# Four edits to a two-layer decoder trunk in emulated fp32: transposes issued together, additions by DMA, two more places with seven products, banks of their own for the last tile

## The chip, the cores and the metric

One core of a Trainium2 chip runs the whole kernel. Its engines are TensorE (PE, with a separate row PEld for loading the stationary operand), VectorE (DVE), ScalarE (ACT), GpSimd (POOL) and SyncE (SP); each executes its own instructions strictly in order. POOL and SP do little here beyond issuing DMAs. A tile framework adds semaphore waits where an instruction needs another engine's result or a buffer that is still being read. The metric is the device time in microseconds of one execution.

## What is computed

256 tokens of width 2048 go through two layers, all in float32. Layer 0 mixes by causal pooling, layer 1 by dilated attention; each is followed by a gated FFN with a causal convolution of width 3 over the tokens. After each part comes a layer norm of the residual sum (post-norm).

```python
def conv_ffn(h, w_up, conv_w, conv_b, w_down):
    u = h @ w_up                                   # 2048 -> 2 * 5504
    up = jnp.pad(u, ((0, 0), (CONV_WIDTH - 1, 0), (0, 0)))
    c = conv_b + up[:, 0:S] * conv_w[0]
    for j in range(1, CONV_WIDTH):
        c = c + up[:, j:j + S] * conv_w[j]
    gate, val = jnp.split(c, 2, axis=-1)
    return (jax.nn.silu(gate) * val) @ w_down      # 5504 -> 2048

for i in range(DEPTH):                             # DEPTH = 2
    mix = pool_mixer(h, ...) if i == 0 else dilated_attention(h, k_shared, v_shared, ...)
    h = layer_norm(DEEPNORM_ALPHA * h + mix, ln1_g[i], ln1_b[i])
    ff = conv_ffn(h, ffn_w_up[i], ffn_conv_w[i], ffn_conv_b[i], ffn_w_down[i])
    h = layer_norm(DEEPNORM_ALPHA * h + ff, ln2_g[i], ln2_b[i])
```

## The kernel before

**Arithmetic.** An fp32 product is made of three products of rounded halves: each operand is split into a high part and the rest, and high·high, high·low and low·high are accumulated. Activations are split once per tile; weights are split as they stream in: ACT casts the high part (`wh`, L99), DVE subtracts to get the low part (`wl`, L100).

**Units.** The program is a list of 435 units, mostly one 512 x 512 block of weights (1 MB) each. `run_units` (L141) does for each unit, in this order: loads up to 5 units ahead and splits up to 3 ahead (`ahead`, L126), copies registered for this unit (`before`), the unit's matmuls, then work that was put off to this unit with `later(n, fn)` (n units on), and the unit's own ending. SP issues all weight loads, into 3 buffers; 4 buffers hold split weights. This program order is the order on every engine, so what a post or a late function issues stands in front of later splits on ACT and DVE.

**The start.** `x_quad` (L532) turns one quarter of x (512 channels) from token-major to channel-major by 8 PE transposes in two halves of 4; after each half ACT copies (L547) and DVE subtracts (L548) to split it, and a copy of H is put off to a later unit. The two halves share one tile of two PSUM banks. Quads 1 to 3 are read in the middle of the first units of `add_in(3)`; quad 0 is read before them, its two halves by separate calls.

**Norms.** With the second norm of layer 0, `shift` (L381) computes the mean over channels of the first part of the residual with PE, ACT copies it to SBUF (L385), and `less` (L405) subtracts it from H[1] to H[3] on DVE, one quarter per unit, H[0] in `one`. Then residual sums arrive (L337), statistics S and Q are collected by DVE (L363 to L369), and `chain` (L424) sums both over the partitions by PE at L425 and L426.

**The FFN.** The hidden width is cut in quarters of 512 channels, q = 0 to 10 (the last has 384). For each, a gate and a value group of 4 units go up; `conv` (L607) makes three taps: ACT scales, DVE adds to `c` (L618); then ACT applies Silu one unit later (L640, `three`), and the product with the value is split (`lo_part`, L304). The down projections go in four chunks (quarters 0–2, 3–5, 6–7, 8–10) and four columns c of 512 outputs, token-major, by `group_tm` (L202). A block of it is multiplied either directly (`go_t`: 24 matmuls of 512 columns) or by seven products of half-blocks instead of eight (`mk_seven`: 42 matmuls of 256 columns in two units, "a" and "b"); the table `sevens` says which quarter and column goes which way. For seven products, `split_sums` (L107) has to form sums of weight blocks by DVE (L120 to L124, three more operations) and splits in two pieces (L113, L114), and at the end of such a column `early_post` (L836) combines the sums: by two DMA additions from POOL into `ht` (L286) or, in the last chunk, by five DVE operations. Layer 0 multiplies the last chunk channel-major (`add_last`), so `sevens[9]` matters only in layer 1.

**The end.** In layer 1 the last column, c = 3 of the last chunk, is `apart`: the first 128 tokens are multiplied first and finished (`finish0`), then the other 128 in two halves of 256 columns (`finish1`). Their accumulators are one new bank "t2" and the second bank of the pair "t". PSUM has 4 pairs of banks (`psp`).

**Attention.** `outputs` (L1097) evacuates two heads at once: one ACT copy, one DVE subtraction (L1110).

## Time and profile before

| | us |
|---|---|
| median of 3 runs | 2026.61 (2026.36 to 2027.33) |
| profiled execution | 2028.4 |
| its span, first to last instruction | 2026.6 |
| granted PE clock, mean | 0.998 of full speed |

| engine | idle just before its costliest groups, us | ended by |
|---|---|---|
| DVE, L100 | 174.6 | ACT, L99 |
| ACT, L99 | 169.0 | PE at L180, 74.6 of it |
| ACT, L113 | 194.7 | mostly DVE, L122 |
| POOL, L286 | 1447.0 | mostly DVE, L869 |

In the chain that ended last PE has 97% and DVE 1%. DMA moves 406.72 MB, 201 GB/s on the mean; its slices vary from 166 to 238 GB/s.

How to read the rows that follow. A row of the waits has the engine and what it was about to run, what it waited for, the total in us, the number of waits and the longest one. A row of the timeline has the start and the duration in us, the engine, line, operation, output and inputs with their form, the number of instructions of which the row is made, and in brackets how long the engine was idle before, and for whom. A row of windows has the limits, the length, the busy time of the engine asked for with its number of instructions, the granted clock, the share of the DMA engines and GB/s. A row of groups ends in total busy time, mean ns of one, and idle time before it with the releaser.

### The profile page before, as it was taken

The numbers are of one execution on the slowest core, as the hardware profiler recorded it, in microseconds if no ns is written. First come the engines' busy times: TensorE is split into PE (matmuls) and PEld (weight loads), VectorE is DVE, ScalarE is ACT, GpSimd is POOL, SyncE is SP. The second block draws the span as 40 slices with busy tenths as digits, with TensorE's granted clock in tenths as the row PEclk, the third lists the DMA queues.
The fourth block names the chain that finished last, engine by engine and source line by source line (L and its number), as shares of the span: only waits on it lengthen the run. The fifth ranks groups of instructions, "written<-read, shape, count | busy, mean of one in ns | idle before, by whom it ended". The sixth has DMA issues, their size and how long they took to land.

```text
span 2026.6 us, 31409 instructions
## 1 busy us (share of the span) xinstructions
PE 2010.2 (99%) x12742; PEld 1812.3 (89%) x12742; DVE 1731.8 (85%) x1823; ACT 1268.6 (63%) x1548; POOL 90.4 (4%) x151
## 2 busy tenths in 40 slices
PE   8999999999999999999999999999999999999998
PEld 7898988999899988889898988998899989989987
DVE  5868887999899989879896878787899899989998
ACT  5554686766776686656553444477767677667672
POOL 2000000000000000000000021000000000000000
PEclk9999999999999999999999999999999999999999
DMA  7655567666656758775565666557666756665765
GB/s 232 214 190 199 167 204 208 177 208 222 214 175 220 234 174 238 216 220 170 190 205 167 197 175 207 187 177 218 167 218 202 225 185 220 208 213 183 218 218 166
DMA packets 270241, 406.72 MB, mean 201 GB/s; under 512 B 74398, under 2 KB 84532, under 8 KB 269840
## 3 DMA queue, kind: packets, MB, share of 16 engines
q1 hardware_dynamic: 259488, 388.93, 58.8%
q0 software_dynamic: 10176, 15.13, 5.0%
q8 instruction: 100, 1.64, 0.3%
q10 hardware_dynamic: 432, 0.66, 0.1%
q14 instruction: 45, 0.37, 0.1%
HBM read 380.01 MB, written 2.10 MB: 189 GB/s over the span
## 4 chain that ended last, share of the span: by engine, by line
PE 97%; DVE 1%; issue 0%; DMA 0%; ACT 0%; SPq 0%; DVEq 0%
PE acc L180 43%; PE acc L181 22%; PE s L244 3%; PE s L242 3%; PE s L243 3%; PE acc L184 3%; PE acc L185 3%; PE acc L183 3%; PE t L244 2%; PE t L242 2%; PE t L243 2%; PE t L253 2%; PE t L254 2%; PE t L255 2%; DVE wl L100 0%
## 5 line engine op out<-in xcount | busy, mean ns | idle before, releaser
L180 PE MATMUL acc<-xc,wh 128*128 128x512 f32 x3264 | 1152.1, 396 | 0.0
L181 PE MATMUL acc<-xc,wl 128*128 128x256 f32 x3264 | 916.0, 281 | 0.0
L100 DVE TENSOR_TENSOR wl<-raw,wh 128x2048 fp32r<-128x2048 f32 (+2 forms) x305 | 657.4, 2163 | 174.6 <-ACT wh L99 172.6
L180 PEld LDWEIGHTS acc<-xc,wh 128*128 128x128 f32 x3264 | 616.0, 189 | 143.6 <-issue 0.3
L99 ACT CAST wh<-raw 128x2048 fp32r<-128x2048 f32 (+2 forms) x305 | 548.6, 1805 | 169.0 <-PE acc L180 74.6
L181 PEld LDWEIGHTS acc<-xc,wl 128*128 128x128 f32 x3264 | 615.4, 189 | 0.1
L113 ACT CAST wh<-raw 128x1024 fp32r<-128x1024 f32 x142 | 148.5, 1052 | 194.7 <-DVE raw L122 175.5
L114 DVE TENSOR_TENSOR wl<-raw,wh 128x1024 fp32r<-128x1024 f32 x142 | 169.4, 1222 | 11.2 <-ACT wh L113 11.2
L121 DVE TENSOR_TENSOR wl<-raw,wh 128x1536 fp32r<-128x1536 f32 x71 | 124.5, 1753 | 6.6 <-ACT wh L119 5.6
L119 ACT CAST wh<-raw 128x1536 fp32r<-128x1536 f32 x71 | 104.9, 1477 | 36.8 <-PE acc L180 28.9
L286 POOL DMA_DIRECT2D ht<-w x48 | 41.3, 1014 | 1447.0 <-DVE ht L869 721.9
L244 PE MATMUL t<-wh,g 128*128 128x256 f32 x376 | 105.7, 281 | 0.0
L242 PE MATMUL t<-wh,g 128*128 128x256 f32 x376 | 105.6, 281 | 0.0
L243 PE MATMUL t<-wl,g 128*128 128x256 f32 x376 | 105.4, 280 | 0.0
L612 ACT ACTIVATE c<-u,cv 128x256 f32<-128x256 f32 x172 | 89.5, 592 | 23.0 <-DVE f L674 16.4
L244 PE MATMUL s<-wh,xs 128*128 128x256 f32 x344 | 96.2, 280 | 0.0
L242 PE MATMUL s<-wh,xs 128*128 128x256 f32 x344 | 96.1, 279 | 0.0
L243 PE MATMUL s<-wl,xs 128*128 128x256 f32 x344 | 96.0, 279 | 0.0
L124 DVE TENSOR_TENSOR raw<-raw 128x1024 f32<-128x1024 f32 x71 | 87.0, 1225 | 2.4
L617 ACT ACTIVATE a<-u,cv 128x256 f32<-128x256 f32 x172 | 73.5, 499 | 11.9 <-DVE g L684 11.9
L603 ACT COPY u<-acc 128x512 f32<-128x512 f32 x84 | 46.8, 572 | 47.1 <-PE acc L181 46.8
L617 ACT ACTIVATE u<-u,cv 128x256 f32<-128x256 f32 x172 | 73.4, 499 | 0.0
(328 smaller groups left out, 3440.4 us busy)
## 6 DMA issues: line engine op xcount, KB each, us to landing
raw<-in_ffn_w_up_dram SPq DMA_DIRECT2D x160, 1024.0 KB, 5.2
raw<-in_ffn_w_down_dram SPq DMA_DIRECT2D x80, 1024.0 KB, 5.1
raw<-in_pool_w_out_dram SPq DMA_DIRECT2D x16, 1024.0 KB, 5.0
raw<-in_shared_w_k_dram SPq DMA_DIRECT2D x16, 1024.0 KB, 5.1
raw<-in_attn_w_q_dram SPq DMA_DIRECT2D x16, 1024.0 KB, 5.3
raw<-in_shared_w_v_dram SPq DMA_DIRECT2D x16, 1024.0 KB, 5.2
raw<-in_attn_w_o_dram SPq DMA_DIRECT2D x16, 1024.0 KB, 5.2
ht<-w POOLq DMA_DIRECT2D x50, 256.0 KB, 4.9
```

The lines of the kernel that those rows point to most:

```text
L99: A.copy(wh[i][:, s], r[:, s])
L100: V.tensor_tensor(wl[i][:, s], r[:, s], wh[i][:, s].bitcast(F32), OP.subtract)
L113: A.copy(h[:, :, n], r[:, :, n])
L114: V.tensor_tensor(l[:, :, n], r[:, :, n], h[:, :, n].bitcast(F32), OP.subtract)
L119: A.copy(hs, rs)
L121: V.tensor_tensor(ls, rs, hs.bitcast(F32), OP.subtract)
L180: PE.matmul(ps[m].ap, h[:, k, c], q[:, k, :, :T], start=st, stop=False)
L181: PE.matmul(ps[m][:, :T], l[:, k, c], q[:, k, 0, :T], start=False, stop=sp)
L242: PE.matmul(to, xh, h[:, k, n], start=opens and kk == 0, stop=False)
L243: PE.matmul(to, xh, l[:, k, n], start=False, stop=False)
L244: PE.matmul(to, xl, h[:, k, n], start=False, stop=ends and kk == 1)
L617: A.activation(to[:, m, :], u[:, m, i:i + T], AF.Copy, scale=cv[:, i, j:j + 1])
```

## The change

1. `x_quad` issues all its transposes first and copies the halves afterwards; H is copied by one ACT operation instead of two.
2. `shift` stores the negated mean, in a tile of its own for the norm in question; `less` becomes a DMA issued by POOL that adds the broadcast mean to H[1], H[2] and H[3] in SBUF, straight at `shift`.
3. Layer 0, quarter 7: the line that kept columns 2 and 3 direct is gone, so all four go by seven products.
4. Layer 1, quarter 9: column 1 too goes by seven products (columns 0 to 2; column 3 remains direct).
5. Layer 1, gates of quarters 8 to 10: the third tap is added to `c` by a POOL DMA instead of DVE.
6. The last tile (`apart`): the pair "t" serves the first 128 tokens alone, and each half of the others gets a new bank "th".
7. `outputs`, last group of heads: one copy and one subtraction per head.

```diff
--- before.py
+++ after.py
@@ -207,7 +207,9 @@
 
         def opened():
             t = pair("t")
-            ps.extend([t[:, 0, :], t[:, 1, :]])
+            ps.append(t[:, 0, :])
+            if not apart:
+                ps.append(t[:, 1, :])
             if seven:
                 t = pair("s")
                 ps.extend([t[:, 0, :], t[:, 1, :]])
@@ -258,8 +260,6 @@
             def go(h, l):
                 if j == 0:
                     opened()
-                    if apart:
-                        ps.append(bank("t2"))
                 held.append((h, l, xqs[j]()))
                 if not apart:
                     for t in range(2):
@@ -270,6 +270,7 @@
                     post(0, ps[0])
                     for half in range(2):
                         c = slice(256 * half, 256 * half + 256)
+                        ps.append(bank("th"))
                         for i in range(j + 1):
                             go_t(*held[i], 1, i, ps[1 + half][:, :256], c)
                         post(1, ps[1 + half], half)
@@ -381,13 +382,16 @@
     def shift(s, first, lay, which):
         ps = bank("shift")
         PE.matmul(ps[:, :T], ones4, s, start=True, stop=True)
-        cs = ST["w4"][:, 3:4, :]
-        A.copy(cs[:, 0, :], ps[:, :T])
+        if first:
+            cs = ST["w4"][:, 3:4, :]
+        else:
+            cs = pools["ffn"].tile([P, 2, T], F32, name="cs", tag="xs", bufs=1)[:, 0:1, :]
+        A.activation(cs[:, 0, :], ps[:, :T], AF.Copy, scale=-1.0)
         cb = cs.to_broadcast([P, 4, T])
         ST["S"] = ST["Q"] = None
 
         def one():
-            V.tensor_tensor(H[0], H[0], cb, OP.subtract)
+            V.tensor_tensor(H[0], H[0], cb, OP.add)
             if first:
                 pre(1)
             stats(0)
@@ -399,16 +403,16 @@
                 pre(3)
 
         def pre(q):
-            V.scalar_tensor_tensor(H[q], H[q], ALPHA, cb, op0=OP.mult, op1=OP.subtract)
+            V.scalar_tensor_tensor(H[q], H[q], ALPHA, cb, op0=OP.mult, op1=OP.add)
 
         def less(q):
-            V.tensor_tensor(H[q], H[q], cb, OP.subtract)
+            nc.gpsimd.dma_start(H[q], cb, accum_op=OP.add)
 
         later(1, one)
         later(2, two)
         if not first:
             for q in (1, 2, 3):
-                later(1 + q, lambda q=q: less(q))
+                less(q)
 
     def xp(q, lay, which):
         g0 = 32 * which
@@ -536,17 +540,21 @@
             XC[q] = quad_tile("xc")
         if halves[0] == 0:
             ST["xT"] = pair("xT")
+        both = ST["xT"]
         for half in halves:
-            ps = ST["xT"][:, half, :]
             for kk in range(2):
                 for t in range(2):
                     k = 2 * half + kk
-                    PE.transpose(ps[:, kk * T + t * P:kk * T + t * P + P], xin[q, t][:, k * P:(k + 1) * P], ident)
-            pv2 = ps.rearrange("p (k t) -> p k t", k=2)
+                    PE.transpose(both[:, half, kk * T + t * P:kk * T + t * P + P], xin[q, t][:, k * P:(k + 1) * P],
+                                 ident)
+        for half in halves:
+            pv2 = both[:, half, :].rearrange("p (k t) -> p k t", k=2)
             s = slice(2 * half, 2 * half + 2)
             A.copy(XC[q][:, s, 0, :T], pv2)
             V.tensor_tensor(XC[q][:, s, 1, :T], pv2, XC[q][:, s, 0, :T].bitcast(F32), OP.subtract)
-            before.setdefault(min(q + 1, 3), []).append(lambda s=s, pv2=pv2: A.copy(H[q][:, s, :], pv2))
+        if halves[-1] == 1:
+            before.setdefault(min(q + 1, 3), []).append(
+                lambda: A.copy(H[q], both.rearrange("p b (k t) -> p (b k) t", k=2)))
 
     def add_in(g, mids=()):
         group(pool_w_in[0], rows4, 512 * g, 512, xsrcs, pool_post(g), mode="a" if g == 3 else "ab", mids=mids)
@@ -582,9 +590,7 @@
         sevens = {q: every for q in range(8)}
         sets = {0: "C", 1: "A", 2: "B", 3: "C", 4: "A", 5: "B", 6: "A", 7: "CB"[lay], 9: "A"}
         if lay == 1:
-            sevens[9] = (0, 2)
-        else:
-            sevens[7] = (0, 1)
+            sevens[9] = (0, 1, 2)
         free, done = {}, {}
 
         def pads():
@@ -604,24 +610,27 @@
                 V.tensor_tensor(y, y, p[:, :n, :T], OP.add)
             return u
 
-        def conv(u, blk0, nb, then, quick=False):
+        def conv(u, blk0, nb, then, quick=False, by_dma=False):
             cv = cvec[lay]
             c = pools["ffn"].tile([P, 4, T], F32, name="c", tag="t4")
             for m in range(nb):
                 j = blk0 + m
                 A.activation(c[:, m, :], u[:, m, 2:], AF.Identity, scale=cv[:, 2, j:j + 1], bias=cv[:, 3, j:j + 1])
 
-            def tap(i, to):
+            def tap(i, to, by_dma=False):
                 for m in range(nb):
                     j = blk0 + m
                     A.activation(to[:, m, :], u[:, m, i:i + T], AF.Copy, scale=cv[:, i, j:j + 1])
-                V.tensor_tensor(c[:, :nb], c[:, :nb], to[:, :nb], OP.add)
+                if by_dma:
+                    nc.gpsimd.dma_start(c[:, :nb], to[:, :nb], accum_op=OP.add)
+                else:
+                    V.tensor_tensor(c[:, :nb], c[:, :nb], to[:, :nb], OP.add)
 
             def second():
                 tap(1, pools["ffn"].tile([P, 4, T], F32, name="a", tag="t4"))
 
             def third():
-                tap(0, u[:, :, 0:T])
+                tap(0, u[:, :, 0:T], by_dma)
                 then(c)
 
             for n, fn in ((1, second), (2, third)):
@@ -642,7 +651,7 @@
 
                     later(1, three)
 
-                later(1, lambda: conv(u, 4 * q, nb, gated))
+                later(1, lambda: conv(u, 4 * q, nb, gated, by_dma=lay == 1 and q > 7))
 
 
 
@@ -1106,8 +1115,10 @@
             PE.matmul(ps[:, :T], vt[:, 0, hd], t[:, :T], start=True, stop=False)
             PE.matmul(ps[:, P:T], vt[:, 1, hd], t[:, T:], start=False, stop=True)
         o = oq[hq][:, ms[0]:ms[0] + 2]
-        A.copy(o[:, :, 0, :T], both[:, :, :T])
-        V.tensor_tensor(o[:, :, 1, :T], both[:, :, :T], o[:, :, 0, :T].bitcast(F32), OP.subtract)
+        for at in (slice(0, 1), slice(1, 2)) if hq == 3 else (slice(0, 2),):
+            hi = o[:, at, 0, :T]
+            A.copy(hi, both[:, at, :T])
+            V.tensor_tensor(o[:, at, 1, :T], both[:, at, :T], hi.bitcast(F32), OP.subtract)
 
     def v_group(hq):
         js = (0, 1, 2, 3)
```

The program now has 438 units instead of 435. The line numbers of the new code are up to 9 higher at the same statements.

How the order of instructions changes, at three places. On PE, the transposes of quad 1 (of its eight, the third to the seventh; `xin` are the loaded tiles of x). Before:

```order
L544 MATMUL xT<-ident,xin_111 128x128
L544 MATMUL xT<-ident,xin_112 128x128
L544 MATMUL xT<-ident,xin_111 128x128 [waits DVE_49]
L544 MATMUL xT<-ident,xin_112 128x128
L544 MATMUL xT<-ident,xin_111 128x128
```

Now:

```order
L548 MATMUL xT<-ident,xin_111 128x128
L548 MATMUL xT<-ident,xin_112 128x128
L548 MATMUL xT<-ident,xin_111 128x128
L548 MATMUL xT<-ident,xin_112 128x128
L548 MATMUL xT<-ident,xin_111 128x128
```

The fifth transpose waited for DVE, which reads the first half; the wait is gone. On ACT, around the Silu of quarter 8 of the second FFN (`u` and `c` are the up-projected tile and the convolved one, `wh` and `raw` split and loaded weights). Before:

```order
L617 ACTIVATE u<-u,cv_672 128x256 [waits Activation_49] x4
L119 CAST wh_17078<-raw_16986 128x2x768 [waits DMAHW7_49,PE_49]
L640 ACTIVATE c<-c 128x1024 [waits DVE_49]
L603 COPY u<-acc 128x2x256 [waits PE_49] x2
L113 CAST wh_17126<-raw_16986 128x4x256 [waits DVE_49] x2
```

Now:

```order
L623 ACTIVATE u<-u,cv_668 128x256 [waits Activation_49] x4
L119 CAST wh_17131<-raw_17039 128x2x768 [waits DMAHW7_49,PE_49]
L649 ACTIVATE c<-c 128x1024 [waits DMASW0_49]
L609 COPY u<-acc 128x2x256 [waits PE_49] x2
L113 CAST wh_17179<-raw_17039 128x4x256 [waits DVE_49] x2
```

Nothing moved, but Silu waits for a DMA's semaphore where it waited for DVE's addition. On DVE, the last 60 us, from the first of the splits around the end of column 0 of the last chunk (`w`, `s` and `ht` are what `early_post` combines). Before:

```order
L100 TENSOR_TENSOR wl_18334<-raw_18247,wh_18333 128x1536 [waits DMAHW1_49,Activation_49]
L304 TENSOR_TENSOR g<-c,g 128x3x256 [waits Activation_49]
L100 TENSOR_TENSOR wl_18361<-raw_18285,wh_18360 128x2048 [waits DMAHW2_49,Activation_49]
L841 TENSOR_TENSOR w<-w,s 128x256 [waits DMASW4_49,DMASW3_49,Activation_49]
L842 TENSOR_TENSOR w<-w,s 128x256 [waits DVE_49]
L849 TENSOR_TENSOR ht<-ht,w 128x512
L851 TENSOR_TENSOR ht<-ht,w 128x512 [waits DVE_49]
L853 TENSOR_TENSOR ht<-ht,s 128x2x256 [waits DVE_49]
L100 TENSOR_TENSOR wl_18398<-raw_18331,wh_18397 128x1536 [waits DMAHW3_49,Activation_49]
```

Now:

```order
L100 TENSOR_TENSOR wl_18385<-raw_18300,wh_18384 128x1536 [waits DMAHW1_49,Activation_49]
L305 TENSOR_TENSOR g<-c,g 128x3x256 [waits Activation_49]
L120 TENSOR_TENSOR raw_18338<-raw_18338 128x2x256 [waits DMAHW2_49]
L121 TENSOR_TENSOR wl_18412<-raw_18338,wh_18411 128x2x768 [waits Activation_49]
L122 TENSOR_TENSOR raw_18338<-raw_18338 128x2x256 [waits DVE_49]
L124 TENSOR_TENSOR raw_18338<-raw_18338 128x4x256 [waits DVE_49]
L850 TENSOR_TENSOR w<-w,s 128x256 [waits DMASW2_49,DMASW1_49,Activation_49]
L851 TENSOR_TENSOR w<-w,s 128x256 [waits DVE_49]
L858 TENSOR_TENSOR ht<-ht,w 128x512
L860 TENSOR_TENSOR ht<-ht,w 128x512 [waits DVE_49]
L862 TENSOR_TENSOR ht<-ht,s 128x2x256 [waits DVE_49]
L114 TENSOR_TENSOR wl_18452<-raw_18338,wh_18451 128x4x256 [waits Activation_49] x2
L100 TENSOR_TENSOR wl_18486<-raw_18409,wh_18485 128x1536 [waits DMAHW3_49,Activation_49]
```

A plain split of a block of quarter 9 (column 1) has become six operations, two of which (L114) now stand behind the five of `early_post`; these five were there already for column 0. Column 1 gets five of its own further on.

## The prediction

> **What bounds the kernel now.** First the page's line of busy times, then the waits of PE, longest total first.
>
> ```profile
> PE 2010.2 (99%) x12742; PEld 1812.3 (89%) x12742; DVE 1731.8 (85%) x1823; ACT 1268.6 (63%) x1548; POOL 90.4 (4%) x151
> ...
> PE xT L544 <- DVE xc L548: 5.2, 4, 1.4
> PE acc L425 <- DVE S L369: 1.2, 1, 1.2
> PE t L253 <- DVE ht L867: 1.1, 1, 1.1
> PE acc L426 <- DVE Q L369: 0.8, 1, 0.8
> PE acc L180 <- DVE o L1110: 0.7, 1, 0.7
> ```
>
> PE is busy in 2010.2 of 2026.6 us. Time can be won in two ways: fewer matmul columns, or these waits (5.2 + 1.2 + 1.1 + 0.8 + 0.7 = 9.0 us). All five wait for DVE, which at 85% has little room. So the question for each edit is whether PE or DVE carries the end of its own stage; the mean over the kernel says nothing about the last 70 us.
>
> **The change part by part.** The profiled execution took 2028.4 us with a span of 2026.6, so 1.8 us lie around the span; the median of the runs shown is 2026.61 (2026.36 to 2027.33), 1.8 below it. I sum changes of the span and add them to the median.
>
> *1. The transposes of x (L532).* The timeline at the second of the three quads that are read during the first units:
>
> ```profile
> 22.08 0.60 PE L544 MATMUL xT<-ident,xin 128*128 128x128 f32 x4
> 22.71 0.59 ACT L547 CAST xc<-xT 128x512 fp32r<-128x512 f32 x1 [3.65 <-PE xT L544]
> 23.33 0.69 DVE L548 TENSOR_TENSOR xc<-xT,xc 128x512 fp32r<-128x512 f32 x1 [4.18 <-ACT xc L547]
> 24.08 0.66 PE L544 MATMUL xT<-ident,xin 128*128 128x128 f32 x4 [1.40 <-DVE xc L548]
> ...
> 10.97:17.80 6.83, 5.43 (x27) 5.03 (x26) 3.13 (x6) 2.96 (x6) 0.00 (x0) 0.50 1.04 382
> ```
>
> Four transposes, then PE idles while ACT and DVE copy the half bank pair, then four more. With all eight issued first, nothing waits between them, and the copies run beside the next matmuls. Three such gaps of 1.40 are 4.2; the fourth wait of the 5.2 (1.0) belongs to quad 0, whose halves are still issued apart, and stays. A gap shown as idle begins at the modelled end of a pipelined transpose: from start to start it is 24.08 − 22.08 = 2.00, and four transposes need about 0.4 of it, so a gap is worth up to 1.6 and three 4.8. I take **−4.8**. The bound on the other side is 0: if the weights of the next unit came only then, PE would wait for them instead. The fifth row is a window over all engines (length, busy time of PE, PEld, DVE, ACT, POOL, then the granted clock): the clock stands at 0.50 from 10.97 to 17.80, and the first gap lies in it. With the gap filled the clock could rise one step of the trace (3.4 us, half that window) earlier, worth half of 3.4 us at half speed: 0 to −1.7. I take **−0.3**, since I can't see what step the gap spoils. By the Trainium skill ("TensorE: Matmul & The Clock Gate", Part 1) the throttle lifts after one busy window of about 3.4 us whose phase is free; that would give any value between these two bounds, and the row does not contradict it.
>
> *2. Quarter 7 of the first FFN, columns 2 and 3 by seven products.* Windows of one direct tile and one seven-product tile (PE alone: length, busy):
>
> ```profile
> 1954.86:1960.44 5.58, 5.58 (x27) 1.00 0.44 158
> 1960.44:1965.39 4.95, 4.95 (x43) 1.00 0.84 287
> ```
>
> A tile by seven products is 0.63 us shorter on PE; two of them −1.3. DVE gets in exchange a split in sums instead of a plain one, which I price in part 6 at +4.4, less a little. DVE there:
>
> ```profile
> 790.00:823.00 33.00, 26.88 (x25) 1.00 0.84 240
> 823.00:850.40 27.40, 23.51 (x24) 1.00 0.81 221
> ```
>
> Of 60.4 us DVE is idle in 10.0, so 8.8 more fit, barely. I take **−1.2**; if they don't fit at the place, the gain is gone (0).
>
> *3. The mean shift before the second norm of layer 0 (L405).* Three DVE subtractions become DMAs that POOL issues and that add in memory; they start as soon as the shift is known.
>
> ```profile
> 894.32 0.37 ACT L385 COPY fold<-shift 128x256 f32<-128x256 f32 x1 [3.46 <-PE shift L383]
> 901.42 0.68 DVE L337 TENSOR_TENSOR h<-h,acc 128x512 f32<-128x512 f32 x1
> L405 DVE TENSOR_TENSOR h<-h,fold x3: 1218/1218/1221, 907.8 to 914.0; 128x1024 f32<-128x1024 f32 x3
> 936.13 0.43 DVE L369 TENSOR_TENSOR S<-S,fold 128x256 f32<-128x256 f32 x1
> 936.61 0.70 PE L425 MATMUL acc<-S,onesd 128*128 128x256 f32 x2 [1.19 <-DVE S L369]
> 937.65 0.42 DVE L369 TENSOR_TENSOR Q<-Q,fold 128x256 f32<-128x256 f32 x1
> ...
> 907.80:938.07 30.27, 29.75 (x42) 1.00 0.62 207
> ```
>
> DVE loses 3 × 1.22 = 3.66 us in a stretch that it works through almost without a pause up to S and Q (the last row, a window of DVE: 29.75 of 30.27 us busy). Those come 3.66 earlier, at 932.9 and 934.4, before PE asks (936.61 − 1.19 = 935.4). Both waits go: 1.2 + 0.8 shown, about 2.3 from start to start; **−2.2**. Condition: the DMA into the quarter that DVE reads first must land in 901.42 − 894.69 = 6.7 us from the shift. Later than that, DVE stands still for the difference.
>
> *4. The price of such a DMA.* No DMA with 512 KB from this queue is in the trace. The nearest are the 256 KB ones from L286:
>
> ```profile
> L286 POOL DMA_DIRECT2D ht<-w x48: 837/1040/1196, 406.0 to 1948.1; - x48
> ...
> DMA to landing us min/median/max: 3.3/5.0/6.2
> ```
>
> Two of them in a row are an issue of 1.0 and a landing of 5.0, so 6.0 for 512 KB. Below: 3.3, the shortest of the 256 KB ones. Above: they have 128 rows of 2 KB each, the new ones 512 rows of 1 KB; if each row costs an issue share of its own, the issue is 4 × 1.04 and the landing 4.2 + 5.0 = 9.2. I take 6.0, with 3.3 to 9.2 kept for the range. The Trainium skill ("DMA: Bandwidth & Descriptors", section "Anatomy of one DMA — SWDGE (gpsimd) path") gives 2.0 us plus the bytes at 436 GB/s, by estimate 3.2 for 512 KB: shorter than any landing of half the size here, so I don't sum by it; with it this DMA would cost nothing on the path, as in rival B. Against the change speaks the Trainium skill ("SBUF — State Buffer", section "SBUF: two separate sides"): while DVE runs an operation that takes both ports, POOL can't write descriptors. The 48 issues above, between 0.84 and 1.20 us beside a DVE at 85%, show no such stall; if it came it would lead to rival C.
>
> *5. Third gate taps of quarters 8, 9, 10 of the second FFN by DMA.* DVE is freed of one addition each (1.2 us), but Silu waits for the landing, in order, on ACT. Quarter 8:
>
> ```profile
> 1830.40 1.70 ACT L617 ACTIVATE u<-u,cv 128x256 f32<-128x256 f32 x4
> 1833.98 1.06 ACT L640 ACTIVATE c<-c 128x1024 f32<-128x1024 f32 x1 [0.51 <-DVE c L618]
> 1836.81 0.58 ACT L603 COPY u<-acc 128x512 f32<-128x512 f32 x1 [1.29 <-PE acc L181]
> 1843.11 2.29 DVE L100 TENSOR_TENSOR wl<-raw,wh 128x2048 fp32r<-128x2048 f32 x1 [1.42 <-ACT wh L99]
> ...
> 1846.50 0.40 PE L180 MATMUL acc<-xc,wh 128*128 128x512 f32 x1
> ```
>
> The taps end at 1832.1, the DMA lands at 1838.1, and Silu starts there instead of at 1833.98: 4.1 late. Queued behind it on ACT are two evacuations and casts of the next weights, for which DVE's L100 waits. ACT's next idle time takes 1.3 of it, and the weights of 1843.11 to 1845.40 are needed by the unit that PE begins at 1846.50, 1.1 later. What is left, 4.1 − 1.3 − 1.1 = 1.7, stalls PE; I take **+1.6**, falling to 0 for a landing of 4.3 us and rising one for one above. At quarter 9 the weights are further ahead: 0. Quarter 10:
>
> ```profile
> 1937.61 1.31 ACT L617 ACTIVATE u<-u,cv 128x256 f32<-128x256 f32 x3
> 1941.34 0.84 ACT L640 ACTIVATE c<-c 128x768 f32<-128x768 f32 x1
> ```
>
> 384 KB are 0.5 to 1 us less: landing at about 1938.9 + 5.6 = 1944.5, Silu 3.2 late. DVE's idle time after that (1.33 in the first window below) takes some; between 0 and 1.9 reaches DVE's queue, **1.0** taken, counted below.
>
> *6. Quarter 9, column 1 by seven products, and the end.* Windows of DVE, then its groups and idle times there:
>
> ```profile
> 1955.00:1976.00 21.00, 19.67 (x21) 1.00 0.65 225
> 1976.00:1997.00 21.00, 19.75 (x22) 1.00 0.57 188
> 1997.00:2014.22 17.22, 16.87 (x32) 1.00 0.29 118
> 1971.10:1973.87 2.77, 2.70 (x6) 1.00 0.88 301
> 1980.50:1987.10 6.60, 6.53 (x7) 1.00 0.31 114
> ...
> L100 DVE TENSOR_TENSOR wl<-raw,wh 128x2048 fp32r<-128x2048 f32 x5 | 11.4, 2289 | 1.6 <-ACT wh L99 1.6
> ...
> 1992.66 4.50 DVE L100 TENSOR_TENSOR wl<-raw,wh 128x2048 fp32r<-128x2048 f32 x2 [1.05 <-ACT wh L99]
> 2016.69 0.42 DVE L872 TENSOR_TENSOR ht<-ht,t 128x256 f32<-128x256 f32 x1 [1.60 <-PE t L255]
> ```
>
> The fourth window is the combination of seven products for one column (2.7), the fifth a split in sums (6.6). A plain split is 2.2 from start to start (4.50 for two). So the change gives DVE 6.6 − 2.2 + 2.7 = 7.1 us in a stretch in which it is busy 94%, 94% and 98%. Behind the place there are two pauses to fill, 1.05 at 1992.66 and 1.60 at 2016.69, and 0.2 of small ones: 7.1 − 2.85 = +4.3, and with the late Silu's 1.0 **+5.3**. PE wins 0.63 there and loses the wait of 1.1 at L253, since the two halves of the last tile now have banks of their own; neither reaches the end, because DVE, in order, takes the last results. Bounds: +3.4 (no delay from Silu, both PE gains felt in part) to +7.1 (pauses not filled).
>
> *7. The third head group's copies by head:* half of the wait of 0.7 at L180, **−0.3**. The negated shift, the one copy of H for two and the banks cost no instruction on PE.
>
> Sum: −4.8 − 0.3 − 1.2 − 2.2 + 1.6 + 5.3 − 0.3 = **−1.9**; 2026.6 − 1.9 = **2024.7**.
>
> **The rivals.** *B, faster:* the DMAs land before ACT comes to Silu (4.3 us or less, between the shortest and the median 256 KB one), and the clock rises a step earlier: −4.8 − 1.7 − 1.2 − 2.2 − 0.3 + 0 + 4.3 = −5.9, 2020.7. For it: landings of 3.3 exist. Against: twice the bytes of the median 5.0.
>
> *C, slower:* the landing is 9.2 by rows of 1 KB. Quarter 8 costs 9.2 − 4.3 = 4.9; quarter 10 about 3.4 in place of 1.0; the shift's DMA is 2.5 late at 901.42, and of −2.2 about −1.0 is left: −4.8 − 0.3 − 1.2 − 1.0 − 0.3 + 4.9 + 4.3 + 3.4 = +5.0, 2031.6. Each us of landing costs about two, so the sum turns positive from 6.9 us and passes 0.2% (4 us) from about 8.7. For it: four times the rows. Against: the issue time is the smaller part of the landing known.
>
> *D, the start does not gain:* the weights of the second to fourth units set the pace and the gaps only change their name. Then −1.9 + 4.8 = +2.9, 2029.5. Against: the gaps end on DVE, with no wait for a load anywhere among PE's longest.
>
> **How the numbers follow.** A measurement of this kernel tells 0.2% (4 us, 2022.6 to 2030.6) from no change. Forecast 0.42 (2021 to 2028 by the bounds of its terms), B 0.30, C 0.18, D 0.10. B is faster by over 0.2% whole, and a tenth of the rest with a better end; C is slower by it nearly whole, and so are some cases of D with a late DMA: faster 0.38, same 0.42, slower 0.20. The range takes B and C to their own values with a little beyond B for a better end, 2018.5 to 2031.5.
>
> **What would show it.** Right: no wait of PE at the transposes of quads 1 to 3; none for S and Q at 935; landings of about 6 us for the new DMAs; a PE wait of 1 to 2 us after quarter 8's Silu; DVE without pauses from 1960 to its last normalisation, and PE waiting for DVE's split weights in the last three units. Wrong: landings below 4.5 or above 8, a wait for weights in the first 30 us, or DVE idle before its last results.

## The result, and the profile after

The changed kernel takes 2052.26 us (median of 4 runs, 2049.74 to 2052.95) against 2026.97 for the kernel before beside it: ratio 1.0121, 95% interval 1.0109 to 1.0133. Its profiled execution has a span of 2050.4, 23.8 more than before. 2024.7 was forecast, 2018.5 to 2031.5 the range.

The page's line of busy times and the waits of PE of the changed kernel, in the columns of those before:

```profile
PE 2019.2 (98%) x12796; PEld 1817.4 (89%) x12796; DVE 1740.9 (85%) x1839; ACT 1273.2 (62%) x1553; POOL 98.2 (5%) x157
...
PE acc L181 <- DVE wl L100: 7.4, 6, 2.4
PE s L245 <- DVE wl L114: 3.0, 4, 0.9
PE gb L948 <- DVE dg L946: 2.9, 1, 2.9
PE shift L384 <- DVE S L367: 2.6, 1, 2.6
PE t L256 <- DVE wl L100: 2.3, 1, 2.3
PE acc L180 <- ACT wh L99: 1.9, 2, 1.4
...
PE acc L183 <- ACT wh L99: 1.0, 1, 1.0
...
PE xT L548 <- DVE xc L554: 0.6, 1, 0.6
```

The three gaps at the transposes are gone. In their place PE waits for split weights (L100, L114, L99) and, at the norms and at the end, for DVE's results. But for the last two rows, these are places where it waited for nothing before. PE is also busy 9 us longer, with fewer columns to multiply; part of this is work at half clock, shown below.

Matching the same units in both traces by program order, and taking the difference of their starts on PE (after less before), shows where the time went:

| at (us, before) | difference, us | what lies between |
|---|---|---|
| 41, unit 4 | −4.6 | start |
| 823, first FFN | −5.2 | quarter 7, column 2 |
| 855 | −4.0 | quarter 7, column 3 |
| 884 | −3.6 | |
| 898 | +0.9 | shift of the second norm |
| 938 | +0.2 | S and Q |
| 1237 | +0.9 | last group of heads |
| 1846 to 1852 | +3.8 to +7.5 | Silu of quarter 8 |
| 1915 | +10.9 | Silu of quarter 9 |
| 1955 | +18.4 | Silu of quarter 10 |
| end | +23.8 | quarter 9's sums, last tile |

The price that was taken from the nearest rows stands in the view of the line that issues the taps' DMAs, and in that of the shift's, after their issue times on POOL:

```profile
L625 POOL DMA_DIRECT2D c<-u x3: 1259/1285/1298, 1833.3 to 1952.2; - x3
...
DMA to landing us min/median/max: 9.3/9.3/10.8
...
L409 POOL DMA_DIRECT2D h<-cs x3: 1285/1700/2132, 894.5 to 896.2; - x3
...
DMA to landing us min/median/max: 10.5/13.2/15.0
```

9.3 to 10.8 us and not 6.0; the bound of 9.2 was too low as well. What stood in the way is in the timelines of POOL and SP, first of the changed kernel at quarter 8, then SP's of the kernel before (three loads, of which the first counts here):

```profile
1833.28 1.30 POOL L625 DMA_DIRECT2D c<-u  x1 [28.98 <-ACT u L623]
1833.72 0.37 SPq L89 DMA_DIRECT2D raw<-in_ffn_w_up_dram  x1
...
1832.84 12.95 SPq L89 DMA_DIRECT2D raw<-in_ffn_w_up_dram  x3
```

SP issues a load of 1 MB of weights 0.44 us after the addition (0.45 and 0.31 at quarters 9 and 10). By the trace's packet records 446 packets of weights, of the 512 that this load has, begin between the issue of quarter 8's addition and its own first packet, 5.30 us after the issue; from there to the landing are 4.0. In the kernel before the load stood at 1832.84, 0.7 us after the end of the taps, so the collision could be seen there. On ACT's timeline at quarter 8:

```profile
1831.28 1.71 ACT L623 ACTIVATE u<-u,cv 128x256 f32<-128x256 f32 x4
1832.89 1.47 ACT L119 CAST wh<-raw 128x1536 fp32r<-128x1536 f32 x1
1842.59 1.06 ACT L649 ACTIVATE c<-c 128x1024 f32<-128x1024 f32 x1 [8.24 <-DMA c<-u]
1843.55 1.06 ACT L609 COPY u<-acc 128x512 f32<-128x512 f32 x2
1844.50 2.00 ACT L113 CAST wh<-raw 128x1024 fp32r<-128x1024 f32 x2
```

ACT stands for 8.24 us in front of Silu. The casts at 1844.50 belong to weights that PE needed at about 1845. Three windows of PE (length, busy, granted clock) show what such a stall brings besides:

```profile
893.27:896.68 3.41, 3.41 (x11) 0.51 0.33 81
1852.42:1855.84 3.42, 3.19 (x10) 0.51 0.62 174
1965.06:1971.89 6.83, 4.91 (x16) 0.50 0.77 166
```

Behind the stalls at the shift, quarter 8 and quarter 10 the clock stood at half for 3.4 or 6.8 us. Each 3.4 us at half speed cost up to 1.7 us, so at most 6.8 in these three.

### The profile page after: what moved, and what is told of

Its sections match the earlier page's. It is cut to its first block, busy times and chain, and to the rows that moved or that the text cites. A ratio compares the mean times of both kernels' runs of the same rounds, so it can differ in the third digit from the quotient of the medians.

```text
span 2050.4 us, 31571 instructions
## 1 busy us (share of the span) xinstructions
PE 2019.2 (98%) x12796; PEld 1817.4 (89%) x12796; DVE 1740.9 (85%) x1839; ACT 1273.2 (62%) x1553; POOL 98.2 (5%) x157
## 5 line engine op out<-in xcount | busy, mean ns | idle before, releaser
L181 PE MATMUL acc<-xc,wl 128*128 128x256 f32 x3264 | 918.6, 281 | 7.4 <-DVE wl L100 7.4
L100 DVE TENSOR_TENSOR wl<-raw,wh 128x2048 fp32r<-128x2048 f32 (+2 forms) x302 | 650.7, 2162 | 170.2 <-ACT wh L99 168.3
L99 ACT CAST wh<-raw 128x2048 fp32r<-128x2048 f32 (+2 forms) x302 | 542.9, 1804 | 167.8 <-PE acc L180 69.7
L181 PEld LDWEIGHTS acc<-xc,wl 128*128 128x128 f32 x3264 | 617.3, 189 | 9.5 <-DVE wl L100 9.3
L113 ACT CAST wh<-raw 128x1024 fp32r<-128x1024 f32 x148 | 154.9, 1052 | 199.2 <-DVE raw L122 174.1
L114 DVE TENSOR_TENSOR wl<-raw,wh 128x1024 fp32r<-128x1024 f32 x148 | 176.6, 1222 | 11.1 <-ACT wh L113 11.0
L246 PE MATMUL t<-wh,g 128*128 128x256 f32 x396 | 111.3, 281 | 0.0
L244 PE MATMUL t<-wh,g 128*128 128x256 f32 x396 | 111.3, 281 | 0.0
L245 PE MATMUL t<-wl,g 128*128 128x256 f32 x396 | 111.0, 280 | 0.0
L245 PE MATMUL s<-wl,xs 128*128 128x256 f32 x362 | 101.6, 281 | 3.0 <-DVE wl L114 3.0
L244 PE MATMUL s<-wh,xs 128*128 128x256 f32 x362 | 101.2, 279 | 0.8 <-ACT wh L113 0.8
L246 PE MATMUL s<-wh,xs 128*128 128x256 f32 x362 | 101.3, 280 | 0.0
L245 PEld LDWEIGHTS t<-wl,g 128*128 128x128 f32 x396 | 74.6, 188 | 0.0
L246 PEld LDWEIGHTS t<-wh,g 128*128 128x128 f32 x396 | 74.5, 188 | 0.0
```

The lines of the kernel that those rows point to most:

```text
L99: A.copy(wh[i][:, s], r[:, s])
L100: V.tensor_tensor(wl[i][:, s], r[:, s], wh[i][:, s].bitcast(F32), OP.subtract)
L113: A.copy(h[:, :, n], r[:, :, n])
L114: V.tensor_tensor(l[:, :, n], r[:, :, n], h[:, :, n].bitcast(F32), OP.subtract)
L181: PE.matmul(ps[m][:, :T], l[:, k, c], q[:, k, 0, :T], start=False, stop=sp)
L244: PE.matmul(to, xh, h[:, k, n], start=opens and kk == 0, stop=False)
```

## The experiments

All edits are to the changed kernel unless another base is named; kernel 4 is the kernel of experiment 4. Medians come with the lowest and highest run. The kernel before, run again beside them, had medians of 2026.5 to 2026.8. The lead of an engine is the time by which its split weights are ready before PE needs them. Where traces are matched, the starts of the same matmuls on PE are compared in two profiled executions.

**1. Taps back to DVE.**

```diff
-                later(1, lambda: conv(u, 4 * q, nb, gated, by_dma=lay == 1 and q > 7))
+                later(1, lambda: conv(u, 4 * q, nb, gated, by_dma=False))
```

> The changed kernel with the third gate taps of quarters 8 to 10 added by DVE again, all else kept. Theory 1 (late landings): in the changed kernel the three additions landed 9.3, 9.3 and 10.8 us after issue, and the distance of its units from the same units of the kernel before grew by 6.6 us behind quarter 8's Silu, by 3.4 behind quarter 9's and by 7.5 behind quarter 10's; so about 17.5 us go and the time falls from 2052.3 to 2035 (2033 to 2038). Rival (DVE lacks time from there to the end, because of quarter 9's sums, whatever brings the taps): DVE gets 3.4 us more work, and the time stays above 2045.

2031.17 (2029.15 to 2035.04): 21.1 less, below the expected interval. The taps are most of the loss, more than the 17.5 read off the trace.

**2. Quarter 9, column 1 direct.**

```diff
-            sevens[9] = (0, 1, 2)
+            sevens[9] = (0, 2)
```

> The changed kernel with quarter 9's column 1 multiplied directly again. Theory 1: the last 70 us are worth what was worked out for them, 4 to 5 us, since DVE's 7.1 us go and its pauses come back: about 2047.5 (2046 to 2049). Rival (the sums are most of the loss): 2040 or less.

2043.38 (2041.21 to 2044.89): 8.9 less, between the two. Of the 10.9 between the two profiled executions, 4.2 lie before 1240, where both kernels run the same program, and about 7 in the last 60 us.

**3. Quarter 7 of the first FFN, columns 2 and 3 direct.**

```diff
             sevens[9] = (0, 1, 2)
+        else:
+            sevens[7] = (0, 1)
```

> The changed kernel with columns 2 and 3 of the first FFN's quarter 7 multiplied directly again. Theory 1: in the changed kernel the units lose 1.1 us at 850 and 4.5 from 880 to 898, because DVE and the buffers of loaded weights lost their lead with the two extra sums; that loss goes and the gain of 1.2 on PE goes too: about 2048 (2046.5 to 2049.5). Rival (the loss between 880 and 898 comes from the shift's DMAs, issued at 894.5): no such gain, 2052 to 2054.

2047.21 (2045.91 to 2049.45): 5.0 less, and no wait of PE for S at the shift any more. The part costs 5 us where 1.2 of gain was forecast.

**4. All four taken back** (1 to 3, and the shift by DVE as in 7).

```diff
-            sevens[9] = (0, 1, 2)
+            sevens[9] = (0, 2)
+        else:
+            sevens[7] = (0, 1)
...
-            nc.gpsimd.dma_start(H[q], cb, accum_op=OP.add)
+            V.tensor_tensor(H[q], H[q], cb, OP.add)
...
-                later(1, lambda: conv(u, 4 * q, nb, gated, by_dma=lay == 1 and q > 7))
+                later(1, lambda: conv(u, 4 * q, nb, gated, by_dma=False))
```

> Of the change only the transposes issued together, the banks of the last tile, the copies by head and the negated shift are left; taps, shift, quarter 7 and quarter 9 as before. Theory 1: the start's gain of 4.6 at unit 4 stays to the end, and the wait of 1.1 at 2007 goes: 2021.5 (2020 to 2023). Rival (gains of the start are eaten by later waits of their own): 2026 to 2027, as before.

2023.40 (2021.55 to 2023.70), ratio to the kernel before 0.9981 (0.9971 to 0.9990): 0.2% faster, clear of the noise but 1.9 us short of what was expected. The four steps taken back one by one (experiments 1, 2, 3 and 7) sum to 36.5; together they give 28.9, so their prices are not independent or not exact.

**5. Taps back and quarter 9's column 1 direct.**

```diff
-            sevens[9] = (0, 1, 2)
+            sevens[9] = (0, 2)
...
-                later(1, lambda: conv(u, 4 * q, nb, gated, by_dma=lay == 1 and q > 7))
+                later(1, lambda: conv(u, 4 * q, nb, gated, by_dma=False))
```

> The changed kernel with the taps by DVE and quarter 9's column 1 direct; quarter 7 and the shift's DMAs stay. Theory: without the late taps the last 70 us cost what the forecast said, 4.3 without delay from Silu: 2031.2 less 4.3, 2027 (2025.5 to 2028.5); what then is left over the kernel with all four taken back, 2023.4, is quarter 7 with the shift, 3 to 4. Rival (the end is dearer, as the 8.9 of the single step back suggests): 2024 or less.

2026.48 (2024.02 to 2028.41). With the taps by DVE, quarter 9's column costs 4.7 by the medians; with the late taps 8.9 (experiment 2). That the late taps make it dearer is not shown: the matched traces lose about 7 us in the last 60 in both pairs (kernels 5 and 1, kernel 2 and the changed kernel), and the runs of kernel 1 spread over 5.9 us.

**6. Silu two units later, for quarters 8 and 9; quarter 10 by DVE.**

```diff
-                    later(1, three)
+                    later(3 if lay == 1 and q in (8, 9) else 1, three)
-                later(1, lambda: conv(u, 4 * q, nb, gated, by_dma=lay == 1 and q > 7))
+                later(1, lambda: conv(u, 4 * q, nb, gated, by_dma=lay == 1 and q in (8, 9)))
```

> The changed kernel, but Silu of quarters 8 and 9 comes two units (8.8 us) later on ACT, and quarter 10's tap is added by DVE. Theory 1 (in-order waiting on ACT): the DMAs land 9.3 us after issue as before, but ACT no longer waits for them, and the time is that with all taps by DVE, 2031.2, or up to 1 us below it (2029.5 to 2032.5). Rival (the DMAs delay other transfers, the weights above all): 2036 or more, with ACT or DVE waiting for loads.

2033.02 (2029.72 to 2034.92). The landings are as late as before or later, but PE waits for nothing there, and ACT for one of them, 2.0 us, where it waited 24.7 for the three of the changed kernel:

```profile
DMA to landing us min/median/max: 9.3/10.5/11.7
```

The median lies 0.5 above the expected interval and within the runs of kernel 1. So it was the waiting in order on ACT, not a burden of the DMAs on other transfers, that cost the time.

**7. The shift by DVE, all three quarters.**

```diff
-            nc.gpsimd.dma_start(H[q], cb, accum_op=OP.add)
+            V.tensor_tensor(H[q], H[q], cb, OP.add)
...
-                less(q)
+                later(1 + q, lambda q=q: less(q))
```

> The changed kernel, but the three subtractions of the mean (as additions of its negative) by DVE one unit after the other. Theory 1 (the first DMA lands 10.5 us after issue and DVE stands for 4.07 us at 905 for it, against 3.66 us of work saved): 2052 within 1.5. Rival (the shift's DMAs bring what was forecast, 2.2): 2054.5; rival (they cost more, by a burden on loads): 2049 or less.

2050.77 (2048.90 to 2053.15), 1.5 below the changed kernel with runs that overlap: no gain from the three DMAs, and a loss that isn't resolved. DVE's timeline in the changed kernel has the reason:

```profile
900.57 0.43 DVE L367 TENSOR_TENSOR Q<-fold 128x256 f32<-128x256 f32 x1
905.07 0.69 DVE L338 TENSOR_TENSOR h<-h,acc 128x512 f32<-128x512 f32 x1 [4.07 <-PE acc L181]
```

DVE stands for 4.07 us before it reads H[1]. The row names PE's L181; but the DMA into H[1], issued at 894.5, landed 10.5 later, at 905.0. 4.07 lost eat the 3.66 saved.

**8. H[1] by DVE, H[2] and H[3] by DMA** (on the base of 4).

```diff
-            V.tensor_tensor(H[q], H[q], cb, OP.add)
+            if q == 1:
+                V.tensor_tensor(H[q], H[q], cb, OP.add)
+            else:
+                nc.gpsimd.dma_start(H[q], cb, accum_op=OP.add)
...
-            for q in (1, 2, 3):
-                later(1 + q, lambda q=q: less(q))
+            less(2)
+            less(3)
+            later(2, lambda: less(1))
```

> The kernel with taps, quarter 7 and quarter 9 as before, and of the shift's subtractions H[1] by DVE, H[2] and H[3] by DMA, which DVE needs only some 12 us later than H[1]. Theory 1: both land in time, DVE has 2.4 us less up to S and Q, and most of the wait of 2.3 there goes: 2023.4 less 1.5 to 2.2, 2021.5 (2020.5 to 2022.3). Rival (a DMA of this kind is a loss wherever it stands): 2023.4 or more.

2020.12 (2019.52 to 2020.59), ratio to the kernel before 0.9964 (0.9950 to 0.9977): the fastest kernel of this study. Its waits of PE, all of them:

```profile
PE warm L1170 <- DVE one L1166: 1.1, 1, 1.1
PE acc L185 <- DVE wl L100: 0.9, 3, 0.4
PE xT L552 <- DVE xc L558: 0.6, 1, 0.6
PE acc L180 <- DVE o L1127: 0.5, 2, 0.3
```

Both waits for S and Q are gone. The same DMAs, landing after 10.6 to 13.2 us, help where their result is needed late enough. The gain of 3.3 is more than kernel 4's two waits of 2.0 in all: the profiled execution of kernel 4 has a window of half clock at the S and Q waits, this one none.

**9. Kernel 8 with column 2 of quarter 7 by seven products.**

```diff
-            sevens[7] = (0, 1)
+            sevens[7] = (0, 1, 2)
```

> The kernel with H[1]'s mean by DVE and H[2], H[3] by DMA (2020.1), with column 2 of the first FFN's quarter 7 by seven products, column 3 direct. Theory: DVE has room for one more set of sums there, and PE's 0.63 is won: 2019.5 (2018.8 to 2020.3). Rival (one set already takes the lead of the units before the norm): 2021 to 2024, with a wait of PE for S at the shift.

2022.12 (2020.42 to 2024.18): 2.0 more, the rival, with its sign in the waits of PE:

```profile
PE shift L384 <- DVE S L367: 2.3, 1, 2.3
```

**10. Contiguous rows for the taps' DMAs.**

```diff
+                flat = lambda y: y.rearrange("p a t -> p (a t)")[:, :nb * T]
+                if by_dma:
+                    to = flat(u).rearrange("p (m t) -> p m t", m=nb)
...
-                    nc.gpsimd.dma_start(c[:, :nb], to[:, :nb], accum_op=OP.add)
+                    nc.gpsimd.dma_start(flat(c), flat(u), accum_op=OP.add)
```

> The changed kernel, but ACT writes the scaled third taps of quarters 8 to 10 without the two-column gaps of the padded tile, so that source and target of each DMA are one piece of 4 KB in every partition (128 rows in place of 512 of 1 KB). Theory 1a (the rows set the landing: the trace shows packets of 1 KB that begin about 5 us after the issue, where the 256 KB DMAs of 128 rows begin after about 1.2): landing 5 to 6.5 us in place of 9.3, quarter 8 costs about 2 us, 9 nothing, 10 about 2 to 3, and the time falls to about 2040 (2037 to 2043). Rival 1b (the bytes, or the adding itself, set it): landing above 8.5 us, time 2049 to 2053.

2048.45 (2046.34 to 2049.82), nearest the rival:

```profile
L628 POOL DMA_DIRECT2D c<-u x3: 842/842/857, 1833.8 to 1950.9; - x3
...
DMA to landing us min/median/max: 8.8/8.8/9.4
```

The issue became 0.44 us shorter, the landing 0.5, and the first packet still came 4.9 us after the issue. The number of rows does not set the landing.

**11. Each of these in two DMAs of at most 256 KB** (on the base of 10).

```diff
-                    nc.gpsimd.dma_start(flat(c), flat(u), accum_op=OP.add)
+                    for z in (slice(0, 2 * T), slice(2 * T, nb * T)):
+                        nc.gpsimd.dma_start(flat(c)[:, z], flat(u)[:, z], accum_op=OP.add)
```

> As the kernel with contiguous third taps, but each addition is issued as two DMAs of 128 rows of 2 KB (the last one 1 KB), the form of the 256 KB additions into ht whose first packet comes 1.4 us after the issue and which land 5.0 after it. There, one DMA of 128 rows of 4 KB still had its first packet 5.1 us after the issue. Theory 1c (the form or size of a DMA sets this delay): first packet after 1.4 to 1.7, both landed about 6 us after the first issue, time 2036 to 2042. Rival 1d (something at this place does, whatever the form): first packet 4.5 us or more after the issue, landing of the later half 9 or more after the first issue, time 2046 to 2051.

2043.47 (2042.38 to 2044.52):

```profile
L629 POOL DMA_DIRECT2D c<-u x6: 841/844/1173, 1828.9 to 1947.3; - x6
...
DMA to landing us min/median/max: 3.5/5.6/10.0
```

Neither theory as it stood. The first half's packets begin 1.4 to 2.0 us after its issue; the second half's, though issued 0.5 to 1.1 us later, only 5.2 to 5.5 after theirs. In the pause of 2.7 to 3.7 us between the two run the packets of the weights' load that SP issued 0.2 us after the second half: the first half was ahead of the load, the second was not. Issuing earlier (the first half needs only two of ACT's taps) took off 5.0 us against kernel 10.

**12. Only the transposes together, with the one copy of H that goes with them** (on the kernel before).

```diff
+        both = ST["xT"]
         for half in halves:
-            ps = ST["xT"][:, half, :]
...
+        for half in halves:
+            pv2 = both[:, half, :].rearrange("p (k t) -> p k t", k=2)
...
```

> The kernel before with the transposes of x issued together and nothing else. Theory: the start's term of the forecast, 4.8 and 0.3 for the clock, less what PE then waits for the split weights of units 1 to 4 (1 to 2.4 us in the traces of the other kernels): 3 to 4 us below the kernel before, so what the kernel with all four taken back gains (3.3) is the start alone. Rival: the start gives at most 2, and banks and copies by head the rest.

2025.07 (2024.20 to 2025.38), ratio 0.9992 (0.9983 to 1.0001): 1.5, the rival. In its profiled execution the span is 3.3 shorter, with no half clock at the start but one window of it, 3.4 us, at the waits for S and Q at 934.

**13 to 15. One tap alone by DMA** (on the base of 4; 8, then 9 and 10 in its place).

```diff
-                later(1, lambda: conv(u, 4 * q, nb, gated, by_dma=False))
+                later(1, lambda: conv(u, 4 * q, nb, gated, by_dma=lay == 1 and q == 8))
```

> The kernel with all four taken back (2023.4), with only quarter 8's third tap by DMA. Theory (the size of the landing alone was wrong): by the forecast's own slope a landing 9.3 us after the issue costs 9.3 less 4.3, 5.0, and 1.7 more where a window of half clock follows: 2028 to 2030.5. Rival (it is dear only together with the others): 2025 or less.

2028.78 (2027.43 to 2030.38): 5.4 more, as expected.

> The same with only quarter 9's tap by DMA. Theory (its cost in the changed kernel, 3.4, comes from leads that quarter 8 had used up): 2023 to 2025. Rival (a landing above 9 us outlasts the lead there too): 2026 or more.

2027.66 (2026.35 to 2031.18): 4.3 more, the rival: the lead at this place covers only a part of the delay. The waits of PE and of ACT there, of this kernel:

```profile
PE acc L181 <- DVE wl L100: 3.6, 3, 2.5
...
ACT c L651 <- DMA c<-u: 10.3, 1, 10.3
```

> The same with only quarter 10's tap by DMA, quarter 9 by seven products in two columns. Theory: Silu 6 us late; the split weights and the value's product wait behind it, 1 to 3 us beyond what DVE's idle time there takes: 2024.5 to 2027. Rival (the 7.5 us of the changed kernel belong to this tap alone): 2029.5 or more.

2027.50 (2026.19 to 2029.97): 4.1 more, above the expected 1.1 to 3.6 and below the rival. The three alone sum to 13.8; together they cost 21.1. That the remaining 7 are interplay is not shown. Matched to kernel 4, the traces give 6.3, 5.3 and 3.7 for the three alone; the changed kernel, matched to kernel 1, loses 6.4, 4.5 and 6.5 at the same places: 15.3 against 17.4. What is dearer together is quarter 10, and its addition landed after 7.8 us alone and after 9.3 in the changed kernel. The medians may hide a part of the single prices, since the traces of these three kernels lack the window of half clock at 934 that kernel 4 has; the rest stays open.

**16. The DMAs a unit after their source is written** (on the base of 6, with Silu another unit later).

```diff
-                    nc.gpsimd.dma_start(c[:, :nb], to[:, :nb], accum_op=OP.add)
+                    later(1, lambda: nc.gpsimd.dma_start(c[:, :nb], to[:, :nb], accum_op=OP.add))
...
-                    later(3 if lay == 1 and q in (8, 9) else 1, three)
+                    later(4 if lay == 1 and q in (8, 9) else 1, three)
```

> As the kernel with the Silu of quarters 8 and 9 two units later and quarter 10 by DVE, but the two DMAs themselves are issued one unit (4.4 us) after ACT has written their source, and Silu another unit later. If the delay of 5.2 us between issue and first packet has to do with a source that ACT has only just written, the first packet comes about 1.4 us after the issue; if not, after 5 again. The time says little: 2030 to 2034 either way.

2031.88 (2030.64 to 2033.52), first packets after 5.5. Inconclusive: POOL has nothing before these DMAs in its queue and waits only for ACT's taps, so a later place in the program issued quarter 8's at the same 1831.04 as in kernel 6.

## Why the prediction was wrong

- **The price of the new DMA (part 4)** is the step that failed. It was put at 6.0 us, as two 256 KB additions in a row, with 9.2 as the far end. It is 9.3 to 10.8. The term that it had at nothing is the wait behind a load of weights. Of the 48 additions into `ht` that served as the nearest row, 45 began within 1.6 us of their issue; the pair at 856.57, with a load under way, began after 2.65 and 2.12. The taps' additions begin after 5.3, behind a load that SP issued 0.3 to 0.45 us later. Without it 512 KB would land after about 5.9 us, an estimate from the 1.85 to the first packet of kernel 1's first addition at the shift and the 4.0 from first packet to landing at quarter 8. So 6.0 was a fair price for a free way. The far end was argued from rows of 1 KB, which experiment 10 refutes as the cause; a landing above 8 us was among the prediction's own signs of being wrong.
- **Quarter 8 (part 5):** mechanism, place and slope were right. By "rising one for one above" 4.3, 9.3 gives 5.0; alone it cost 5.4 by the medians and 6.3 by the matched traces, in the changed kernel 6.6, with a window of half clock behind it in either kernel. Mis-sized by its landing, and by the clock, which was in no term.
- **Quarter 9: "the weights are further ahead: 0"** was wrong by itself, +4.3 alone. With ACT standing for 10.3 us the lead there doesn't suffice. **Quarter 10:** 1.0 forecast, 4.1 alone.
- **The taps together** cost 21.1 instead of 2.6. The prediction added them up; how much of the loss is interplay stays open (experiments 13 to 15).
- **The end (part 6):** the mechanism was right. By the medians of kernels 1 and 5 it cost 4.7 for the forecast 4.3; by the matched traces about 7, near the bound of 7.1. DVE works almost without a pause, and PE waits for it three times (0.9, 2.3 and 2.9), with a window of half clock of 3.41 us behind the last:

```profile
1973.30:1994.30 21.00, 19.78 (x23) 1.00 0.49 169
1994.30:2015.30 21.00, 19.99 (x27) 1.00 0.47 157
2015.30:2038.00 22.70, 21.91 (x33) 1.00 0.42 157
```

- **Quarter 7 (part 2):** sign wrong. "Of 60.4 us DVE is idle in 10.0, so 8.8 more fit, barely" counted idle time where lead counts: the sums come in one piece, PE waits 0.9 and 0.5 for split weights at 843 and 847, DVE and ACT reach the norm late, and PE waits 2.6 for S at the shift. One column costs 2.0, two 5.0. The stated worst case, 0, left out that a lost lead is passed on to the next wait.
- **The shift (part 3):** the condition was stated, land within 6.7 us, or "DVE stands still for the difference"; with 10.5 it stood for 4.07 and the 2.2 were gone; PE still waits 0.5 for S and 0.8 for Q. With H[1] left to DVE the step is worth 3.3.
- **The start (part 1):** the gaps went and the clock stayed up, −4.6 at unit 4 in the trace; in time alone 1.5, with an interval that reaches no change. In the trace of kernel 12 a window of half clock at 934, which the kernel before did not have, takes 1.5 of the 4.6 back. Of the rest, 1.8 belongs to the trace of the kernel before, whose profiled execution was that much above its median. Nor does the clock stay up in every kernel with this start: kernels 1, 15 and 16 show a window of half clock of 3.41 us that begins at 11.3 to 12.5.
- **The copies by head (part 7):** −0.3 forecast. PE waits twice for the copies, 0.5 in all, in place of one wait of 0.7, so about −0.2. The +0.7 in the table at 1237 has another source: a pause of 0.4 before L1115, which kernels 1 to 6 don't show.
- **The list of waits** that the prediction starts from leaves out two of more than 1 us, 1.4 at L183 for ACT's cast and 1.1 at the first matmul. No term rests on them, but not all of PE's waits were for DVE.
- **The rivals:** C was the right one, with its place and its sign, and too cheap: 2031.6 where 2052.3 came. Its row argument was wrong, and it gave quarter 9 nothing, the clock nothing and quarter 7 the forecast's gain. The way to C by DVE's ports, weighed in part 4 from the Trainium skill ("SBUF — State Buffer", section "SBUF: two separate sides"), isn't what the runs show: in the changed kernel the first packets came 5.30, 5.34 and 5.35 us after the three issues by the trace's packet records, whatever DVE ran meanwhile. At quarter 9, 0.4 us after the issue at 1888.24, DVE paused for 1.11 us, and the packets came no earlier:

```profile
1889.77 2.29 DVE L100 TENSOR_TENSOR wl<-raw,wh 128x2048 fp32r<-128x2048 f32 x1 [1.11 <-ACT wh L99]
```

What the 5 us between issue and first packet are, the packet records of all kernels tell: the place of SP's next load. Issued 0.16 to 0.46 us after an addition of 384 or 512 KB, it holds the first packet back to 4.9 to 5.6 us; issued 0.3 to 0.5 before it, to 3.9 to 4.1 (kernels 3, 7, 8 and 15). At the shift, where ACT has just written the source as well, the first packet comes after 1.85 us if the load is issued 1.01 later (kernels 1, 2, 6, 9, 11 and 16), and after 3.1 to 4.0 if it is issued 0.8 to 0.9 later (the changed kernel, 5 and 10). So it is not the number of rows, not the size alone and not the fresh source. Open: why a load that is issued later gets ahead. No experiment moved the load alone.

## What to carry to other kernels

Price a moved addition by a measured transfer of the same form at the same place: look in the trace for the loads that are issued within a microsecond of it, since one of them made the difference between about 6 us (the estimate above) and 9.3 here. Then ask who stands behind its consumer in an in-order queue: 9 us of latency cost at most 2 where Silu came two units later, and 5 where it stood in front of the next weights' cast. Idle time of an engine is not lead: one set of sums fitted the idle time and still made PE wait at the next norm. Steps need not add up: the three taps cost 13.8 one by one and 21.1 together by the medians, and only a part of this difference could be found in the traces.

## What was not expected of the hardware

- A load issued by SP up to 0.46 us after an addition issued by POOL went ahead of it: 446 of 512 packets at quarter 8. The taps' additions of 384 or 512 KB began 3.9 to 5.6 us after their issue and landed after 7.8 to 11.7, with rows of 1 KB or of 3 to 4 KB alike. A packet of 2 KB that adds took 0.18 to 0.19 us in the median of the records, one of the weights' loads 0.084.
- A wait of PE of 2.6 us was enough for a window of 3.41 us at clock 0.51 right behind it. The Trainium skill ("TensorE: Matmul & The Clock Gate", Part 1) speaks of at least one idle window of about 3.4 us before the clock drops; by the row at the shift, PE idled less than that here. Whether a stall of about 2 us is followed by such a window changes from kernel to kernel: the waits for S and Q brought none in the kernel before, and one in kernels 4 and 12. Windows of PE in the kernel before, in kernel 4, then in 12:

```profile
938.00:942.00 4.00, 3.87 (x30) 1.00 0.05 18
```

```profile
934.00:938.00 4.00, 4.00 (x23) 0.63 0.00 2
```

```profile
934.00:938.00 4.00, 4.00 (x21) 0.57 0.01 5
```

So one stall of 2 us costs 2 in one kernel and about 1.5 more in another, and differences of 2 us between kernels are not all due to the edit.
